# Interleaving two tensors on one core: loads and stores dealt to two DMA rings in another way

## The chip, the cores and the metric

The kernel runs on one core of one Trainium2 chip. The metric is the device time of one execution in microseconds (us). Before the change it is 314.18 us, the median of 3 runs (314.1 to 314.26).

## What is computed

```python
batch, seq, dim = 32, 256, 1024
result = np.zeros((batch, seq, dim * 2), dtype=np.float32)
result[..., 0::2] = x
result[..., 1::2] = y
```

Two fp32 tensors of 32 x 256 x 1024 (33.55 MB each) are interleaved element by element into an output of 67.11 MB. Nothing is calculated: 67.11 MB are read from HBM, put in a new order and 67.11 MB are written.

## The kernel before

**Tiles.** The work is cut into n = 8 tiles. Tile k takes 128 x 8192 elements (4.19 MB) of x and as many of y, one contiguous row of 32 KB for each of the 128 partitions, and gives 8.39 MB of output, in two halves h = 0 and 1 of 4.19 MB. SBUF holds two buffers for x (`xt[0]`, `xt[1]`), two for y (`yt`), used by tiles k in turn (k % 2), and two for the output (`ot`), one for each half: `ot[0]` takes the first half of every tile and `ot[1]` the second.

**Weaving.** VectorE (DVE) puts a half together with two copies of 128 x 4096: L67 writes x's values at the even places of `ot[h]`, L70 y's at the odd places. It goes through tiles and halves in order, so a tile has four copies. Each copy adds 1 to the semaphore `woven`, so that 4k + 2h + 2 means that half h of tile k is ready. Before L67 of tile k and half h, DVE waits for x (`xsem`, and `hsem` for the second half of x's first tile, which is loaded in two pieces), and, from tile 1 on, for `osem[h]` to reach 16k: the store of the same half of the tile before must have left `ot[h]`. Before L70 of half 0 it waits for y (`ysem`).

**Loads.** SyncE (SP) issues all of them. x's first tile goes in two halves (L42, L43), moved ahead of the opening barrier. Then come, for each tile, x (L50) and y (L53), so y0, x1, y1 right after the barrier. From tile 2 on, x waits until `woven` is 4(k-2)+3 (the last copy that reads the buffer's old x is done) and y until it is 4(k-2)+4.

**Stores.** ScalarE (ACT) issues all of them: for each half it waits until `woven` is 4k + 2h + 2 and issues the store (L83). The first half of tile 0 goes as two stores, a quarter (L77, counted by `qsem`) and three quarters (L81). Each issuing engine has a ring of its own, in which its DMAs are worked off in order: SP's is q1 in the profile and ACT's q10. So q1 carries 67.11 MB of loads and q10 67.11 MB of stores.

**The end.** ACT waits for `osem[0]` and clears the semaphores (L90); SP waits for `osem[1]`, the very last store (L91).

Of the kernel before, what the change touches and what calls it, by code (L numbers as in the profile page):

```python
# [3 lines left out]


def _interleave(nc, x, y, out):
    P = 128
    W = 8192
    H = W // 2  # L10

    total = 1
    for s in x.shape:
        total *= s
    n = total // (P * W)
    assert n * P * W == total

    def rows(ap, names, k):
        flat = ap.rearrange("b s d -> (b s d)")
        return flat[k * names : (k + 1) * names].rearrange("(p w) -> p w", p=P)  # L20

    fp32 = mybir.dt.float32
    xt = [nc.alloc_sbuf_tensor(f"xt{b}", [P, W], fp32).ap() for b in (0, 1)]
    yt = [nc.alloc_sbuf_tensor(f"yt{b}", [P, W], fp32).ap() for b in (0, 1)]
    ot = [nc.alloc_sbuf_tensor(f"ot{b}", [P, W], fp32).ap() for b in (0, 1)]

    xsem = [nc.alloc_semaphore(f"xsem{b}") for b in (0, 1)]
    hsem = nc.alloc_semaphore("hsem")
    qsem = nc.alloc_semaphore("qsem")
    ysem = [nc.alloc_semaphore(f"ysem{b}") for b in (0, 1)]  # L30
    woven = nc.alloc_semaphore("woven")
    osem = [nc.alloc_semaphore(f"osem{b}") for b in (0, 1)]


    cuts = [0, W // 4, W]
    parts = [slice(a, b) for a, b in zip(cuts, cuts[1:])]

    xs = [rows(x, P * W, k) for k in range(n)]
    ys = [rows(y, P * W, k) for k in range(n)]
    os_ = [rows(out, 2 * P * W, k) for k in range(n)]  # L40

    nc.sync.dma_start(out=xt[0][:, :H], in_=xs[0][:, :H]).then_inc(xsem[0], 16)  # L42
    nc.sync.dma_start(out=xt[0][:, H:], in_=xs[0][:, H:]).then_inc(hsem, 16)  # L43

    for k in range(n):
        b = k % 2
        if k >= 2:
            nc.sync.wait_ge(woven, 4 * (k - 2) + 3)
        if k:
            nc.sync.dma_start(out=xt[b], in_=xs[k]).then_inc(xsem[b], 16)  # L50
        if k >= 2:
            nc.sync.wait_ge(woven, 4 * (k - 2) + 4)
        nc.sync.dma_start(out=yt[b], in_=ys[k]).then_inc(ysem[b], 16)  # L53

    for k in range(n):
        b = k % 2
        for h in (0, 1):
            c = slice(h * H, (h + 1) * H)
            if h == 0:
                nc.vector.wait_ge(xsem[b], 16 * (k // 2 + 1))  # L60
            elif k == 0:
                nc.vector.wait_ge(hsem, 16)
            if k:
                nc.vector.wait_ge(osem[h], 16 * k)
            if (k, h) == (1, 0):
                nc.vector.wait_ge(qsem, 16)
            nc.vector.tensor_copy(out=ot[h][:, 0::2], in_=xt[b][:, c]).then_inc(woven, 1)  # L67
            if h == 0:
                nc.vector.wait_ge(ysem[b], 16 * (k // 2 + 1))
            nc.vector.tensor_copy(out=ot[h][:, 1::2], in_=yt[b][:, c]).then_inc(woven, 1)  # L70

    for k in range(n):
        for h in (0, 1):
            nc.scalar.wait_ge(woven, 4 * k + 2 * h + 2)
            if (k, h) == (0, 0):
                for c in parts[:-1]:
                    nc.scalar.dma_start(  # L77
                        out=os_[k][:, c], in_=ot[h][:, c]
                    ).then_inc(qsem, 16)
                c = parts[-1]  # L80
                nc.scalar.dma_start(out=os_[k][:, c], in_=ot[h][:, c]).then_inc(osem[h], 16)  # L81
                continue
            nc.scalar.dma_start(  # L83
                out=os_[k][:, h * W : (h + 1) * W], in_=ot[h]
            ).then_inc(osem[h], 16)

    nc.scalar.wait_ge(osem[0], 16 * n)
    used = sorted(s.num for s in [*xsem, hsem, qsem, *ysem, woven, osem[0]])
    assert used == list(range(used[0], used[-1] + 1)), used
    nc.scalar.sem_clear(range(used[0], used[-1] + 1))  # L90
    nc.sync.nop(nofuse=True).wait_op(osem[1], 16 * n, "sem-ge").then_inc(  # L91
        osem[1], -16 * n
    )


def kernel(tc, x, y, out):
    nc = tc.nc
    tc.close()
    tc.compile()

    _interleave(nc, x, y, out)

    blocks = nc.main_func.blocks
    for engine in (mybir.EngineType.SP, mybir.EngineType.SP):
        opening = blocks[0].instructions
        at, moved = next(
            (b, i)
            for b in blocks[1:]
            for i in b.instructions
            if i.engine == engine and i.opcode == "DMACopy"  # L110
        )
        assert not (moved.sync_info and moved.sync_info.on_wait)
        body = at.instructions
        body.remove(moved)
        gate = next(
            n
            for n, i in enumerate(opening)
            if i.engine == engine and i.opcode == "Drain"
        )
        opening.insert(gate, moved)  # L120
        at.instructions = body
        blocks[0].instructions = opening


# [1 line left out]
_INS = ['x', 'y']  # L126
_OUTS = [((32, 256, 2048), 'float32')]


# [23 lines left out]
```

## Time and profile before

| what | value |
|---|---|
| time, median of 3 runs | 314.18 us |
| span of the profiled execution | 312.9 us |
| around the span (median less span; the profiled execution has no time of its own on record) | about 1.3 us |
| bytes moved | 134.22 MB, mean 429 GB/s over the span |
| DVE | 72.0 us busy (23%), 32 copies of 2.29 us |
| DVE idle before L67, waiting for stores | 206.5 us in 14 waits |
| share of 16 engines' span: q1 (SP), q10 (ACT) | 50.1%, 49.7% |

A DMA here is 128 rows, spread over the core's 16 DMA engines, 8 rows for each engine. The profile counts a row as a packet (8, 16, 24 or 32 KB), and 16 small ones for each DMA besides: 34 DMAs x (128 + 16) = 4896 packets. "DMA share" in a stretch is the mean busy share of the 16 engines. A packet is counted where it starts, so the rate in a short stretch is rough.

### The profile page before, as it was taken

To read this page: it belongs to the slowest core of one execution; us is meant where nothing else is said; L and a number is where in the kernel's file an instruction comes from. 1 tells how busy PE (TensorE), PEld (TensorE's weight loads), DVE (VectorE), ACT (ScalarE), POOL (GpSimd) and SP (SyncE) were. 2 spreads that over 40 slices of the span, in tenths; PEclk is the share of its full clock that TensorE was granted. 3 is DMA by queue.
4 is the path that set the end of the run, shared out by engine and by line. 5 is a ranking of instruction groups with operands and counts; after the bars stand their busy time and mean duration, and the time that the engine had idled before them with its cause. 6 is when DMAs were issued, how large, how long until landed. Compare 5 with 4: busy or idle time off the path is not lost.

```text
span 312.9 us, 114 instructions
## 1 busy us (share of the span) xinstructions
DVE 72.0 (23%) x32; POOL 0.2 (0%) x4
## 2 busy tenths in 40 slices
DVE  0216000501305023050220503205032050415410
POOL 0000000000000000000000000000000000000000
DMA  8999999999999999999999999999999999999998
GB/s 337 467 402 436 436 402 419 452 457 415 427 444 411 461 402 469 402 469 402 469 402 465 406 440 432 423 448 402 469 402 469 402 469 402 469 402 448 423 423 381
DMA packets 4896, 134.22 MB, mean 429 GB/s; under 512 B 544, under 2 KB 544, under 8 KB 544
## 3 DMA queue, kind: packets, MB, share of 16 engines
q1 hardware_dynamic: 2448, 67.11, 50.1%
q10 hardware_dynamic: 2448, 67.11, 49.7%
HBM read 67.11 MB, written 67.11 MB: 429 GB/s over the span
## 4 chain that ended last, share of the span: by engine, by line
DMA 82%; DVE 12%; issue 0%
DMA out_dram<-ot 76%; DMA yt<-in_y_dram 6%; DVE ot L70 6%; DVE ot L67 6%
## 5 line engine op out<-in xcount | busy, mean ns | idle before, releaser
L67 DVE COPY ot<-xt 128x4096 f32<-128x4096 f32 x16 | 36.7, 2295 | 213.8 <-DMA out_dram<-ot 206.5
L70 DVE COPY ot<-yt 128x4096 f32<-128x4096 f32 x16 | 36.6, 2288 | 12.3 <-DMA yt<-in_y_dram 12.3
L137 POOL MEMSET const-bfloat16-1.0<- 128x1 bf16 x1 | 0.1, 103 | 0.0
L137 POOL MEMSET const-uint8-127<- 128x1 uint8 x1 | 0.1, 102 | 0.0
L137 POOL MEMSET const-float32-0.0<- 128x1 f32 x1 | 0.1, 100 | 0.2 <-issue 0.2
L137 POOL MEMSET const-float32-1.0<- 128x1 f32 x1 | 0.1, 99 | 0.0
## 6 DMA issues: line engine op xcount, KB each, us to landing
out_dram<-ot ACTq DMA_DIRECT2D x15, 4096.0 KB, 34.1
yt<-in_y_dram SPq DMA_DIRECT2D x8, 4096.0 KB, 41.5
xt<-in_x_dram SPq DMA_DIRECT2D x7, 4096.0 KB, 24.3
xt<-in_x_dram SPq DMA_DIRECT2D x2, 2048.0 KB, 9.5
out_dram<-ot ACTq DMA_DIRECT2D x1, 3072.0 KB, 32.8
out_dram<-ot ACTq DMA_DIRECT2D x1, 1024.0 KB, 16.3
```

The lines of the kernel that those rows point to most:

```text
L67: nc.vector.tensor_copy(out=ot[h][:, 0::2], in_=xt[b][:, c]).then_inc(woven, 1)
L70: nc.vector.tensor_copy(out=ot[h][:, 1::2], in_=yt[b][:, c]).then_inc(woven, 1)
L137: nc = _bacc.Bacc("TRN2", target_bir_lowering=False, num_devices=1)
```

## The change

The diff deals DMAs to the two rings by tensor and half, and no longer by direction. SP issues x's loads and the stores of half 0; ACT issues y's loads and the stores of half 1. On each engine the order is load k+1, store k, for k = 0 to 7. The waits' thresholds for loads and stores stay. The last tile isn't woven into `ot` but into `xt[0]` and `yt[0]`, the input buffers of tile 6, and so DVE waits there for its own last copy of tile 6 (`woven` at 28) and not for the stores of tile 6. The copies, the buffers, the tile size and the two small stores at the start stay.

```diff
+    nc.scalar.dma_start(out=yt[0], in_=ys[0]).then_inc(ysem[0], 16)
+
+    spare = (xt[n % 2], yt[n % 2])
+
+    def woven_to(k, h):
+        return spare[h] if k == n - 1 else ot[h]
+
+    def store(engine, k, h):
+        engine.wait_ge(woven, 4 * k + 2 * h + 2)
+        if (k, h) == (0, 0):
+            for c, sem in zip(parts, (qsem, osem[h])):
+                engine.dma_start(out=os_[k][:, c], in_=ot[h][:, c]).then_inc(sem, 16)
+            return
+        engine.dma_start(out=os_[k][:, h * W : (h + 1) * W], in_=woven_to(k, h)).then_inc(
+            osem[h], 16
+        )
+
+    def load(engine, t, sem, rows_, k, last):
+        if k >= 2:
+            engine.wait_ge(woven, 4 * (k - 2) + last)
+        engine.dma_start(out=t[k % 2], in_=rows_[k]).then_inc(sem[k % 2], 16)
 
     for k in range(n):
-        b = k % 2
-        if k >= 2:
-            nc.sync.wait_ge(woven, 4 * (k - 2) + 3)
-        if k:
-            nc.sync.dma_start(out=xt[b], in_=xs[k]).then_inc(xsem[b], 16)
-        if k >= 2:
-            nc.sync.wait_ge(woven, 4 * (k - 2) + 4)
-        nc.sync.dma_start(out=yt[b], in_=ys[k]).then_inc(ysem[b], 16)
+        if k + 1 < n:
+            load(nc.sync, xt, xsem, xs, k + 1, 3)
+            load(nc.scalar, yt, ysem, ys, k + 1, 4)
+        store(nc.sync, k, 0)
+        store(nc.scalar, k, 1)
 
     for k in range(n):
         b = k % 2
...
-            if k:
+            if k == n - 1:
+                nc.vector.wait_ge(woven, 4 * k)
+            elif k:
                 nc.vector.wait_ge(osem[h], 16 * k)
             if (k, h) == (1, 0):
                 nc.vector.wait_ge(qsem, 16)
-            nc.vector.tensor_copy(out=ot[h][:, 0::2], in_=xt[b][:, c]).then_inc(woven, 1)
+            nc.vector.tensor_copy(out=woven_to(k, h)[:, 0::2], in_=xt[b][:, c]).then_inc(woven, 1)
             if h == 0:
                 nc.vector.wait_ge(ysem[b], 16 * (k // 2 + 1))
-            nc.vector.tensor_copy(out=ot[h][:, 1::2], in_=yt[b][:, c]).then_inc(woven, 1)
-
-    for k in range(n):
-        for h in (0, 1):
-            nc.scalar.wait_ge(woven, 4 * k + 2 * h + 2)
...
-            nc.scalar.dma_start(
-                out=os_[k][:, h * W : (h + 1) * W], in_=ot[h]
-            ).then_inc(osem[h], 16)
+            nc.vector.tensor_copy(out=woven_to(k, h)[:, 1::2], in_=yt[b][:, c]).then_inc(woven, 1)
```

On the engines this means: DVE has the same 32 copies in the same order; ACT issues 16 DMAs where it had 17 (8 loads and 8 stores); SP issues 18 where it had 17 (9 loads of x, 9 stores).

More of the change, by code (lines that the diff above doesn't have):

```diff
@@ L66, in _interleave @@
                 nc.vector.wait_ge(qsem, 16)
-            nc.vector.tensor_copy(out=ot[h][:, 0::2], in_=xt[b][:, c]).then_inc(woven, 1)
+            nc.vector.tensor_copy(out=woven_to(k, h)[:, 0::2], in_=xt[b][:, c]).then_inc(woven, 1)
             if h == 0:
                 nc.vector.wait_ge(ysem[b], 16 * (k // 2 + 1))
-            nc.vector.tensor_copy(out=ot[h][:, 1::2], in_=yt[b][:, c]).then_inc(woven, 1)
-    for k in range(n):
-        for h in (0, 1):
-            nc.scalar.wait_ge(woven, 4 * k + 2 * h + 2)
[L75 to L83, printed above, removed]
-                out=os_[k][:, h * W : (h + 1) * W], in_=ot[h]
-            ).then_inc(osem[h], 16)
+            nc.vector.tensor_copy(out=woven_to(k, h)[:, 1::2], in_=yt[b][:, c]).then_inc(woven, 1)
     nc.scalar.wait_ge(osem[0], 16 * n)
```

## The prediction, as it was put on record

> **What bounds the kernel now.** I read the page's DMA rows first, then the chain, then the rate stretch by stretch, then the timeline at the two ends.
>
> ```profile
> DMA  8999999999999999999999999999999999999998
> DMA packets 4896, 134.22 MB, mean 429 GB/s; under 512 B 544, under 2 KB 544, under 8 KB 544
> q1 hardware_dynamic: 2448, 67.11, 50.1%
> q10 hardware_dynamic: 2448, 67.11, 49.7%
> DMA 82%; DVE 12%; issue 0%
> ```
>
> The 16 DMA engines are busy in every slice; the two rings together take 99.8% of the span. The chain names DVE for 12%, but only because a store follows a copy: while those copies run, the other ring and the store before keep the engines busy, as these stretches show (length, busy time of DVE and POOL, clock, DMA share, GB/s):
>
> ```profile
> 12.20:26.60 14.40, 4.69 (x3) 0.00 (x0) 1.00 1.01 437
> 26.60:32.60 6.00, 2.01 (x1) 0.00 (x0) 1.00 0.93 366
> 58.00:270.40 212.40, 49.04 (x22) 0.00 (x0) 1.00 1.01 434
> 293.50:303.20 9.70, 4.50 (x2) 0.00 (x0) 1.00 1.00 432
> ```
>
> The first has loads alone on one ring, the third loads and stores on two, the last stores alone on one. All move 432 to 437 GB/s: direction and the number of rings make no difference here. Only the second, where the stores begin, is slower. So the bound is bytes over a rate that stands still. From the chain:
>
> ```profile
> 115.53 0.02 issue
> 154.25 0.02 issue
> 192.98 0.02 issue
> ```
>
> A tile of 16.78 MB (four DMAs) takes 38.72 us, so one DMA 9.68 us and one packet of 32 KB on one engine 38.72 / 32 = 1.21 us.
>
> **Where the span's other time is.** x0 and y0 (8.39 MB) have landed at 21.89 us. Two DMAs at 9.68 are 19.36, so 2.5 us go to the start: the first issue, the ramp and the first landing. The other 30 DMAs take 312.9 - 21.9 = 291.0 us and would take 30 x 9.68 = 290.4 at the steady rate: 0.6 us are lost, and the stretch 26.6:32.6 says where. Span = 2.5 + 32 x 9.68 + 0.6 = 312.9. (34 issues, but three are pieces: 32 times 4.19 MB.)
>
> **The change, part by part.**
>
> 1. *Bytes, packets, copies.* The same DMAs of the same shapes and the same 32 copies. 0.
>
> 2. *Issues.* ACT takes eight loads, SP nine stores. An issue is 0.33 to 0.46 us (timeline rows of SP and ACT). Each lies behind a wait for `woven` and ahead of a ring that still holds other work, so 0; without such work it would cost its own 0.4 us. The stores' new waits on SP (4k+2) have x of tile k+2 queued behind them, which waits for 4k+3 anyway; on ACT the store and y behind it wait for the same 4k+4. Neither wait delays an issue by itself.
>
> 3. *The new order in each ring.* SP: x0 (two pieces), x1, s00 (two pieces), x2, s10, x3, s20, ...; ACT: y0, y1, s01, y2, s11, y3, .... It costs something only when both rings are empty at once. How the rings share is seen in the stretch 31:40, where SP's ring held loads and ACT's the quarter store:
>
> ```profile
> q1 hardware_dynamic: 107, 2.98, 77.5%
> q10 hardware_dynamic: 107, 0.79, 20.7%
> ```
>
> As many packets of each, whatever their size. So I follow the rings packet by packet, an engine having 8 of each DMA (0.61 us for 16 KB, 0.3 for 8, 0.91 for 24, 1.21 for 32). At about 3 us (SP's first issue after the barrier is at 1.90, and x0's first packets come 1 us after theirs, the rate in the first us being 16 GB/s) y0 joins x0's first piece, which has 7 packets left: 7 pairs of 1.82 us, it lands at 15.7; y0 lands at 17. x0's second piece (16 KB) pairs with y1 and lands at about 30, y1 at 31.4. The first half is woven at about 20; its store waits in the ring behind x1. The second half can be woven only at 30 to 34.7. ACT's ring is empty from 31.4 to 34.7, but SP's has x1. Then s01 and y2 pair with x1 (to 46), s00's quarter (8 pairs of 1.51, to 58) and its rest; y2 is in at about 65.6, s00 at 70.2. ACT's ring is empty again, and x2 runs alone from 70.2 to 79.9. Meanwhile tile 1 is woven: four copies, 9.0 us, 70.2 to 79.2; s10 is issued after two of them at 74.7, s11 and y3 at 79.2. So SP's ring goes over from x2 to s10 at 79.9 without a hole.
>
> From there both rings run in step: s1, then x3 and y3 (19.4 us, the cover of the 9.0 us of weaving), s2, and so on: 24 DMAs x 9.68 = 232.3 us to 312.2, plus what the stores' start loses. Cost of the order: 0.
>
> 4. *The last tile in `xt[0]`, `yt[0]`.* Now x7 and y7 land together, at about 273, and s60, s61 run until about 292 with nothing behind them if tile 7 had to wait for `ot`. That would leave both rings dry for two copies, 4.5 us. With the free buffers tile 7 is woven at 273 to 282, and s70, s71 are queued 10 us ahead. So this edit earns nothing against before, where the second-last store covers the weaving (next fence): it takes away a cost of 4.5 us which edit 3 makes.
>
> ```profile
> 283.90 2.30 DVE L67 COPY ot<-xt 128x4096 f32<-128x4096 f32 x1 [8.95 <-DMA out_dram<-ot]
> 286.11 2.29 DVE L70 COPY ot<-yt 128x4096 f32<-128x4096 f32 x1
> 293.53 2.29 DVE L67 COPY ot<-xt 128x4096 f32<-128x4096 f32 x1 [5.14 <-DMA out_dram<-ot]
> ```
>
> The store of tile 7's first half is issued at 288.4 and its forerunner lands at 293.5: there was never a hole.
>
> 5. *The stores' start, 0.6 us.* The trace can't tell whether it belongs to the first use of ACT's ring, which now falls into the ramp (then -0.6, up to -0.8 if y0 helps the ramp as well), or to the first stores (then 0, they still start), or to any ring that starts again from empty (ACT's at 34.7 and 79.2: +0.6). I take 0, the middle, and keep -0.8 and +0.6.
>
> 6. *The end.* ACT's clearing of semaphores follows s70, which lands no later than s71 since SP's ring began first; 0, or about 0.1 us if the two land together.
>
> **Sum:** 312.9 + 0 = 312.9 span, + 1.3 around it = 314.2 us, the median before.
>
> **The rivals.**
>
> *Faster: 0.13.* The start loss goes with the early first use of ACT's ring and the ramp shrinks: 314.2 - 0.8 = 313.4. For it: the loss stands where ACT's ring is first used. Against: the rate of 432 to 437 in all other stretches leaves nothing else to gain.
>
> *Slower, a hole at 80 us: 0.15.* Mechanism: s10 starts late, and x2, alone in the rings, ends before it. It decides when s10's first packet comes more than 79.9 - 74.7 = 5.2 us after its issue. The one store in the trace issued while DVE was still weaving speaks for it: L77 at 24.24, and q10 has no packet in the stretch 24.2:28.6; the copies end at 28.6.
>
> ```profile
> 24.24 0.38 ACTq L77 DMA_DIRECT2D out_dram<-ot  x1
> 24.64 0.46 ACTq L81 DMA_DIRECT2D out_dram<-ot  x1
> 26.32 2.29 DVE L70 COPY ot<-yt 128x4096 f32<-128x4096 f32 x1
> ```
>
> If 4.4 us is a delay from the issue, s10 comes at 79.1, in time by 0.8 us. If stores wait for DVE's copies, it comes at 79.2, in time by 0.7. If the 4.4 us follow the copies, it comes at 83.6: 3.7 us lost, 317.9. A smaller miss gives 315 to 316.
>
> *Slower, two loads side by side: 0.10.* Before, x and y never load at the same time. Now x and y of one tile do, row for row, in nearly all of the loading. If this is slower than 433 GB/s, some 12 DMAs (50.3 MB) pay: at 413, the rate of the stretch 27:42, 121.9 in place of 116.2 us, +5.7, so 320; at 366, the slowest row above, +21, so 335. Against it: the rate stood still whatever was mixed, and the 16 engines read 16 rows at once already.
>
> The Trainium skill, "DMA: Bandwidth & Descriptors", in "Latency and other measured facts", speaks for this rival: copies whose rows lie a large power of two apart fell to half of the rate (103 against 207 GB/s each way at 4 MiB), and x and y are each 2^25 bytes long. No run here shows it; by its halving, those 50.3 MB would cost an estimated 116 us more.
>
> **How the numbers follow.** Forecast, no change: 0.62, at 314.2. Faster 0.13, the hole 0.15, two loads 0.10. A difference of 0.2% (0.63 us) is about what a measurement of this kernel tells from none. Faster by more than that is 0.13; slower is 0.15 + 0.10 = 0.25; within is 0.62. The range goes from 313.4 (the faster case) to 316.4, which holds item 5's +0.6 and the smaller holes; it leaves out the two loads (0.10) and the large hole (about 0.05).
>
> **What would show it.** Right: DMA at 9 in every slice; s10 landing near 99 us; then a landing of stores every 38.7 us; the stores' ends at 309 to 313. The hole: a slice near 80 us with a lower digit, and later landings shifted by it. Two loads: periods of more than 38.7 us, the excess in the stretches in which both rings load. Faster: no stretch below 430 GB/s where the stores begin. The forecast is wrong if both rings are empty anywhere, or if the rate depends on what the two rings carry.

## The result, and the profile after

In twelve executions each, the kernel before takes 314.25 us in the median (314.10 to 314.46) and the changed kernel 322.41 us (314.84 to 327.01). The ratio is 1.0076, with a 95% interval of 1.0050 to 1.0103; it leaves out the six of the twelve executions that were over 1.5% longer than its shortest. What the change brings first of all is thus a spread: the same program takes 314.9 us once and 326 the next time, where the kernel before stays within 0.4 us; in 49 more executions of it, timed beside the runs below, it takes 314.10 to 314.45 us.

The profiled execution is one of the short ones: 314.94 us, span 313.6. Its page, in the lines that answer to those of before:

```profile
DMA  8999999999999999999999999999999999999997
DMA packets 4896, 134.22 MB, mean 428 GB/s; under 512 B 544, under 2 KB 544, under 8 KB 544
q1 hardware_dynamic: 2592, 67.11, 50.1%
q10 hardware_dynamic: 2304, 67.11, 49.6%
DMA 77%; DVE 11%; another core or an unknown queue 2%; issue 0%; SPq 0%; DVEq 0%
```

Full in every slice, with the two rings at 99.7% of the span. Both rings carry the same bytes; q1 has 2 x 144 more packets (both pieces of x's first tile and both of the first store). The chain, in which a tile's last store releases DVE (start, length, what):

```profile
103.97 0.03 issue
...
142.73 0.02 issue
...
181.49 0.02 issue
```

A tile takes 38.76 us here, against 38.72. A long stretch in the middle, in the windows' columns (length, DVE, POOL, clock, DMA share, GB/s), moves as much as before:

```profile
100.00:290.00 190.00, 50.84 (x23) 0.00 (x0) 1.00 1.00 433
```

The place of the hole that the prediction feared, in the timeline and in the DMA queues of the stretch 72:80 (packets, MB, share):

```profile
71.75 2.30 DVE L87 COPY ot<-xt 128x4096 f32<-128x4096 f32 x1 [41.70 <-DMA out_dram<-ot]
73.95 2.29 DVE L90 COPY ot<-yt 128x4096 f32<-128x4096 f32 x1
76.16 2.29 DVE L87 COPY ot<-xt 128x4096 f32<-128x4096 f32 x1
76.27 0.33 SPq L57 DMA_DIRECT2D out_dram<-ot  x1
```

```profile
DMA packets 104, 3.41 MB, mean 426 GB/s; under 512 B 0, under 2 KB 0, under 8 KB 0
## 3 DMA queue, kind: packets, MB, share of 16 engines
q1 hardware_dynamic: 104, 3.41, 98.6%
```

x2 is alone in the rings, as forecast (72 to 81 us, forecast 70.2 to 79.9); the store of tile 1's first half is issued at 76.27 and lands at 96.8, and there is no hole. And the last tile, woven into the free buffers while tile 6 is still being stored:

```profile
271.24 2.30 DVE L87 COPY xt<-xt 128x4096 f32<-128x4096 f32 x1 [7.64 <-DMA xt<-in_x_dram]
278.55 2.29 DVE L90 COPY xt<-yt 128x4096 f32<-128x4096 f32 x1 [5.01 <-DMA yt<-in_y_dram]
280.76 2.29 DVE L87 COPY yt<-xt 128x4096 f32<-128x4096 f32 x1
```

So from 46 us on this execution went much as the prediction worked it out (y2 lands at 69.5 us against 65.6, the rest is closer). Before that it did not: y0's first packets start at 5.7 to 6.4 us, not at 3, and the first landings are 4 to 8 us off (x0's first piece 10.9 us against 15.7 forecast, y0 20.7 against 17, x0's second piece 25.5 against 30, y1 39.5 against 31.4). No ring runs dry there, so the sum did not feel it. The execution is 0.7 us longer than before. Worked out from the packets' starts and durations, as the rates below are that stand outside the fences, 392 GB/s are moved in the stretch 35 to 45 us, where the stores begin: a loss of 0.95 us against 0.58 before. The three tiles from 104 to 220 us take 38.76, 38.76 and 38.84 us, 0.2 us more together. What makes the median 8 us longer isn't in it.

### The profile page after: what moved, and what is told of

It is laid out like the page before. It is cut to its first block, busy times and chain, and to the rows that moved or that the text cites. A ratio compares the mean times of both kernels' runs of the same rounds, so it can differ in the third digit from the quotient of the medians.

```text
span 313.6 us, 114 instructions
## 1 busy us (share of the span) xinstructions
DVE 72.0 (23%) x32; POOL 0.2 (0%) x4
## 4 chain that ended last, share of the span: by engine, by line
DMA 77%; DVE 11%; another core or an unknown queue 2%; issue 0%; SPq 0%; DVEq 0%
DMA out_dram<-ot 56%; DMA xt<-in_x_dram 15%; DMA yt<-in_y_dram 6%; DVE ot L87 4%; DVE ot L90 4%; DVE xt L87 1%; DVE xt L90 1%; DVE yt L90 1%; DVE yt L87 1%; SPq L55 0%; DVEq L86 0%
## 5 line engine op out<-in xcount | busy, mean ns | idle before, releaser
L87 DVE COPY ot<-xt 128x4096 f32<-128x4096 f32 x14 | 32.1, 2295 | 193.1 <-DMA out_dram<-ot 179.7
L90 DVE COPY ot<-yt 128x4096 f32<-128x4096 f32 x14 | 32.0, 2289 | 7.5 <-DMA yt<-in_y_dram 7.5
L87 DVE COPY xt<-xt 128x4096 f32<-128x4096 f32 x1 | 2.3, 2296 | 7.6 <-DMA xt<-in_x_dram 7.6
L90 DVE COPY xt<-yt 128x4096 f32<-128x4096 f32 x1 | 2.3, 2295 | 5.0 <-DMA yt<-in_y_dram 5.0
L87 DVE COPY yt<-xt 128x4096 f32<-128x4096 f32 x1 | 2.3, 2287 | 0.0
L90 DVE COPY yt<-yt 128x4096 f32<-128x4096 f32 x1 | 2.3, 2286 | 0.0
```

Source lines behind the costliest of these rows:

```text
L87: nc.vector.tensor_copy(out=woven_to(k, h)[:, 0::2], in_=xt[b][:, c]).then_inc(woven, 1)
L90: nc.vector.tensor_copy(out=woven_to(k, h)[:, 1::2], in_=yt[b][:, c]).then_inc(woven, 1)
```

## Experiments

Below, the *lag* is the time between the first and the last of the 16 landings of one DMA: each of the 16 DMA engines adds 1 to the DMA's semaphore when its part has landed, and the trace has the time of each.

### A longer execution: again_1 and again_2

No edit; two more executions of the changed kernel, with their profiles.

> The changed kernel once more, to see one execution's stretches. Its 12 times lie between 314.8 and 327.0 us, and the one profiled took 314.9 and kept 433 GB/s in all stretches but the start of the stores. If a stretch has both rings empty (the hole), this execution shows a low DMA share there, some us at one place, and 9.68 us for each DMA elsewhere. If loads or stores side by side are slow, the tile's period grows evenly (from 38.7 to about 40 us for a time of 325), and the excess lies in the stretches where both rings load (or both store).

> The same kernel as again_1, a second look, with the same expectations: a hole is one place with a low DMA share; a slower rate is a longer period in every tile. If it takes 315 us, it shows nothing new.

326.34 and 326.36 us. The page of again_1:

```profile
span 325.0 us, 114 instructions
...
DMA  9999999999999999999999999999999999999951
...
q1 hardware_dynamic: 2592, 67.11, 48.5%
q10 hardware_dynamic: 2304, 67.11, 48.1%
```

There is no hole: the digits are full until the 38th slice, and then fall to 5 and 1. The windows around that place:

```profile
100.00:290.00 190.00, 46.94 (x22) 0.00 (x0) 1.00 1.00 430
290.00:313.00 23.00, 5.42 (x3) 0.00 (x0) 1.00 0.96 416
313.00:324.00 11.00, 0.00 (x0) 0.00 (x0) 1.00 0.12 51
```

For 313 us, the time in which the other execution is done, this one is nearly as busy (430 against 433 GB/s in the long window). Then 11 us follow at a share of 0.12: two of 16 engines (0.125) still work, and the rest have nothing left. Here is how tiles 3 to 6 go (DVE's first copy of each):

```profile
138.53 2.29 DVE L87 COPY ot<-xt 128x4096 f32<-128x4096 f32 x1 [30.01 <-DMA out_dram<-ot]
...
180.11 2.29 DVE L87 COPY ot<-xt 128x4096 f32<-128x4096 f32 x1 [31.10 <-DMA out_dram<-ot]
...
221.92 2.30 DVE L87 COPY ot<-xt 128x4096 f32<-128x4096 f32 x1 [30.86 <-DMA out_dram<-ot]
...
263.34 2.29 DVE L87 COPY ot<-xt 128x4096 f32<-128x4096 f32 x1 [31.43 <-DMA out_dram<-ot]
```

41.4 to 41.8 us for a tile and not 38.7: DVE waits for the slowest engine's part of each store. The landings show the rest: in both executions the lag on SP's ring is 0.7 to 0.9 us at 81 us, 2.0 at 98, and grows with every DMA to 13 at 284 us, with one or two engines behind and fourteen within 0.5 us of each other. The records don't name the engines, but the packets of again_1 can be strung together into 16 chains that leave no gaps; fourteen end at 312.6 to 313.1 us and two at 323.8 and 324.6. From 60 us on 64 packets of 32 KB took more than 1.23 us, up to 2.42; in the short execution 13 did, up to 1.35, and in the kernel before one, 1.25. What the 64 took beyond 1.21 us adds up to 24 us, about what the two late engines lose together (11 and 12): longer packets are their delay, and no waiting.

What follows: neither of the two expectations. There is no hole and no stretch that is slow for all engines; some packets are held up, most of all on one or two engines, and these fall behind.

### Is it loads, or stores, side by side? loads_two and stores_two

loads_two has three buffers each for x and y, leaves out the weaving, and stores one tile alone:

```diff
+    for k in range(2 * n):
+        load(nc.sync, xt, xsem, xs, k, k % n)
+        load(nc.scalar, yt, ysem, ys, k, (k + 0) % n)
```

stores_two loads one tile, leaves out the weaving, and then stores:

```diff
+    for k in range(n):
+        nc.sync.dma_start(out=os_[k][:, :W], in_=xt[0]).then_inc(osem[0], 16)
+        nc.scalar.dma_start(out=os_[k][:, W:], in_=yt[0]).then_inc(osem[1], 16)
```

> Loads alone: each of x and y is loaded twice over, x by SP's ring and y by ACT's side by side, three buffers each, so that each ring always has work; no weaving, and only two stores of 4.19 MB at the end (the output is left unwritten but for one tile). 32 loads and 2 stores at 9.68 us are 329 us, and about 332 to 333 with the start and the last landings. By the theory that two loads side by side are slow, it takes over 340 us, or its times spread by some per cent from one execution to the next as the changed kernel's do; by the others (a hole, two stores side by side) it takes 332 with a spread under 0.3%.

> Stores alone: one tile of x and of y is loaded, and then all 16 halves of the output are stored from these two buffers, half 0 by SP's ring and half 1 by ACT's, side by side (nothing is woven, the output is not interleaved). 2 loads and 16 stores at 9.68 us are 174 us, about 177 with start and end. By the theory that two stores side by side are slow, it takes over 180 us or its times spread by some per cent; by the others 177 with a spread under 0.3%.

336.7 to 337.0 us and 181.7 to 181.9 us: 4 and 5 us over the figure, and neither spreads. stores_two is also over the 180 us that were to speak for slow stores, so its rate has to decide. The middle stretch of loads_two, and then that of stores_two:

```profile
23.30:314.70 291.40, 0.00 (x0) 1.00 1.00 430
```

```profile
42.90:179.00 136.10, 0.00 (x0) 1.00 1.00 431
```

A pair of loads lands every 19.43 us and a pair of stores every 19.44: 9.72 us for a DMA, 0.4% more than the 9.68 of mixed work, and no engine falls behind (the lag is 0.6 us at 62 us and at 315). A part of the rest is the wait between the loads and the first store that needs them, which the figures left out (1.2 to 1.8 us in stores_two, in which the engines stand still); another is the start, as the first pair lands at 23 us. What follows: the rival of slow loads side by side is out, and that of slow stores. The power-of-two rule of the Trainium skill ("DMA: Bandwidth & Descriptors", "Latency and other measured facts"), weighed in the prediction, does not show here: x and y side by side load at 430 GB/s. How far apart the two lie in memory no trace shows.

### One ring loading while the other stores: out_of_phase

New theory (switch): engines are held up where all of them go over from loading to storing, or back, on both rings at about the same time.

```diff
-    cuts = [0, W // 4, W]
+    cuts = [0, W]
...
+        elif t is yt:
+            engine.wait_ge(xsem[1], 16)
         engine.dma_start(out=t[k % 2], in_=rows_[k]).then_inc(sem[k % 2], 16)
...
```

> The changed kernel with the first store whole and with y's second tile held back until x's second has landed, so that from about 29 us on one ring loads while the other stores. The order of DMAs in each ring stays. Theory (switch): two of the 16 DMA engines fall behind by about 1.5 us in each tile where all engines go over from storing to loading on both rings at once; with one ring loading and one storing at all times, as before the change, nobody falls behind: 313.5 to 315 us, a spread under 0.3%, and the 16 landings of each DMA within 0.6 us to the end. Rival (a ring that carries both directions in turn disturbs): times still spread from 315 to 327.

314.64 to 314.94 us in eight of ten executions, and 315.42 and 316.52; ratio to before 1.0023 (1.0012 to 1.0035).

```profile
DMA  9999999999999999999999999999999999999998
```

```profile
50.00:290.00 240.00, 60.91 (x28) 0.00 (x0) 1.00 1.01 434
```

The lag is 0.6 us at 56 us and at 313. Two of the ten are over the 315 us that were expected. But for the first store, which is whole here, the rings carry the same DMAs in the same order as in the changed kernel. What follows: that a ring carries both directions in turn is not enough to make the spread. Two things were changed, though, the phase and the first store, and the kernel with the whole store alone (whole_store, below) is as steady in eight of ten; this run doesn't tell the two apart, and the runs with two engines set back have to. Nor is the phase wholly opposite. SP's ring turns at 87.1, 106.5 and 125.8 us and ACT's at 94.4, 113.7 and 133.1, so the rings go in opposite directions for 12 of each 19.4 us and in the same one for 7. In the changed kernel ACT's ring also turns 7 us after SP's (104.0 after 96.8, 123.4 after 116.1), but the same way: both load or both store for 12 us, and for 7 they are mixed. The 0.5 us that it is behind the kernel before stand where the stores begin (387 GB/s from 25 to 35 us, 1.07 us lost against 0.58).

### Turning on one ring: one_ring

```diff
-    nc.scalar.dma_start(out=yt[0], in_=ys[0]).then_inc(ysem[0], 16)
+    nc.sync.dma_start(out=yt[0], in_=ys[0]).then_inc(ysem[0], 16)
...
-            load(nc.scalar, yt, ysem, ys, k + 1, 4)
+            load(nc.sync, yt, ysem, ys, k + 1, 4)
         store(nc.sync, k, 0)
-        store(nc.scalar, k, 1)
+        store(nc.sync, k, 1)
...
```

> The changed kernel's order of DMAs, all on SP's ring: loads of x and y, then both stores, in turn; ACT issues none. Every engine still goes over from loading to storing and back every 19.4 us. By the switch theory two engines fall behind here as well, and the times lie above 317 or spread by over 1%. By the rival that it takes two rings side by side, nobody falls behind: pure stretches cost 9.72 a DMA (loads_two, stores_two), so 32 x 9.72 + 3 = 314 to 315.5, spread under 0.3%.

315.55 to 318.17 us, six executions, median 317.14. In the profiled one (317.35) the lag grows from 0.7 us at 110 us to 3.0 at 287, with two to four engines behind. This fits neither expectation well: a lag, but a quarter of that of again_1, and three of six times above 317. It shows where packets are held up: 52 of its 54 that took more than 1.23 us after 60 us start within 2 us of the landing of the first part of a load of y (80.5, 119.2, 158.0, 196.8, 235.5, 274.3 us), where the ring goes from loads to stores.

### The first store in one piece: whole_store

```diff
-    cuts = [0, W // 4, W]
+    cuts = [0, W]
...
```

> The changed kernel with the first store in one piece of 4.19 MB and not in 1.05 and 3.15. The pieces put SP's ring 7 us ahead of ACT's in the changed kernel, so that 7 of each 19.4 us are mixed; whole, the rings should go over more nearly together. Switch theory: engines still fall behind, times from 315 to 330 with a spread over 1%. Rival (the stragglers come from the 8 KB packets of the small store): 314 to 315 with a spread under 0.3%.

314.70 to 315.06 us in eight of ten executions, and 316.53 and 317.93; ratio 1.0034 (1.0013 to 1.0055). The one profiled is the longest, and its lag grows from 0.5 us at 83 to 6.1 at 299. So the stragglers are there without the 8 KB packets, but much rarer and slower to grow, and the expectation missed on that. With the whole store no ring runs alone around 75 us, and ACT's ring is about 5 us ahead of SP's and not 7 behind.

### Without the free buffers: no_spare

```diff
-        return spare[h] if k == n - 1 else ot[h]
+        return ot[h]
...
-            if k == n - 1:
-                nc.vector.wait_ge(woven, 4 * k)
-            elif k:
+            if k:
```

> The changed kernel with the last tile woven into ot, as before, so that its copies wait for tile 6's stores. In the trace of the changed kernel SP's ring is 7 us ahead of ACT's at the end (stores of tile 6 land at 290.6 and 297.9), so that SP's ring is empty while ACT's still has work; ACT's is empty while SP's store of tile 7 runs. By the prediction's item 4 a hole of up to 4.5 us; with the 7 us between the rings, each covers the other, so 0 to 2 us. The spread of the changed kernel stays (315 to 328).

317.24, 317.47, 319.06, 329.16 and 330.25 us. The shortest is 2.4 us over the changed kernel's shortest. The profile is of the longest, in which one engine lags by 13 us:

```profile
285.00:305.00 20.00, 1.45 (x1) 0.00 (x0) 1.00 0.41 175
```

Before the last tile the other fifteen engines run out of work and wait until the straggler has landed its part of tile 6's store. So the free buffers are worth 2.4 us to this order, if the two shortest executions can be compared, and in a long one 328.9 - 325.0 = 3.9 us of span. The prediction had 4.5. All five executions are on one chip, and they spread like the changed kernel's.

### Setting two engines back: seed_after, seed_out_of_phase, seed_before, seed_loads

If being out of step is what costs, then an engine that is put out of step must pay in every execution. Two rows of a DMA fall on two engines:

```diff
+    R = 2
...
+    spill = nc.alloc_sbuf_tensor("spill", [P, 4000], fp32).ap()
...
+        if k == 1:
+            for r in range(R):
+                nc.sync.dma_start(out=spill[2 * r : 2 * r + 2], in_=xs[0][2 * r : 2 * r + 2, :4000]).then_inc(ssem, 16)
...
```

> The changed kernel with two small extra loads behind the store of tile 1's first half, each of two rows of 16,000 bytes into a scratch tile that nothing reads; with two rows they should fall on two of the 16 engines only and set these back by 2 x 0.6 = 1.2 us at about 100 us. Switch theory: an engine that is out of step with the others is held up each time the others turn, so the two fall further behind in every execution: lag growing from 1.2 us to 8 us and more, all times above 319. Rival (chance stalls that have nothing to do with being out of step): 1.2 us more than the changed kernel, spread between 316 and 328 as before, and the lag stays at 1.2 us where the execution is a short one.

> The same two extra loads in out_of_phase, where one ring loads while the other stores. Switch theory: the lag of 1.2 us stays as it is to the end, 315.9 to 316.2 us in nearly all runs. If any lagging engine is slowed whatever the others do, it grows to several us, 319 and more.

> The same two extra loads in the kernel before, on SP's ring behind y's fourth tile. Switch theory: loads and stores are mixed on all engines at all times, the lag of 1.2 us stays to the end: 315.4 to 315.6 us, spread under 0.3%. If any lagging engine is slowed whatever the others do: 319 and more.

> The same two extra loads in loads_two, behind its sixth pair of loads: a pure stream of loads on two rings, in which nothing turns until the end. Switch theory: the lag of 1.2 us stays, 338.1 us. If a lagging engine is slowed in a pure stream as well, the landings of one DMA drift apart from 1.8 us to several us by 310 us.

| kernel | without the two loads, us | with them, us |
|---|---|---|
| changed kernel | 314.84 to 327.01 | 325.82 to 327.74 |
| out_of_phase | 314.64 to 316.52 | 316.27 to 316.55 |
| before | 314.10 to 314.46 | 317.77 to 319.89 |
| loads_two | 336.73 to 337.03 | 338.87 to 338.92 |

The page and the end of seed_after:

```profile
DMA  9999999999999999999999999999999999999951
...
q1 hardware_dynamic: 2600, 67.17, 48.6%
q10 hardware_dynamic: 2304, 67.11, 48.0%
```

```profile
313.00:324.00 11.00, 0.00 (x0) 0.00 (x0) 1.00 0.12 51
```

These are the rows of again_1 once more, and now all four executions are as long as it. The lag of the DMA on SP's ring that lands nearest to each time, in us:

| kernel | at 80 us | 120 | 165 | 205 | 245 | 285 |
|---|---|---|---|---|---|---|
| before | 0.2 | 0.3 | 0.2 | 0.2 | 0.2 | 0.2 |
| after, the short execution | 0.4 | 0.4 | 0.5 | 0.6 | 0.6 | 0.6 |
| again_1 | 0.7 | 2.6 | 4.9 | 7.9 | 10.3 | 13.2 |
| seed_after | 0.5 | 6.8 | 9.0 | 11.7 | 14.0 | 14.0 |
| seed_out_of_phase | 1.8 | 6.8 | 6.7 | 6.6 | 6.6 | 6.5 |
| seed_loads | 0.5 | 0.5 | 6.2 | 6.2 | 6.2 | 6.2 |
| seed_before | 0.4 | 0.4 | 6.9 | 7.6 | 8.0 | 8.6 |

The first jump is larger than 1.2 us because the extra packets take their turns against ACT's, the small one that ends each DMA too: the two rows on an engine start 3 to 4 us apart, time for a row and two packets of 1.21. So the two engines fall about 6 us behind on SP's ring and get 1 to 3 us ahead on ACT's. What they cost by themselves is read from seed_loads and seed_out_of_phase, 2.0 and 1.6 us, and not 1.2. What counts is what happens after: in a pure stream of loads the lag stands still for 150 us, and with the rings in opposite phase as well; in the changed kernel it goes on growing, on ACT's ring too (1.6 us at 163, 10.1 at 286), and costs 11.5 us over a short execution. In the kernel before it grows a little, and costs 3.5 to 5.6 us, more than the 1.2 that was expected: an engine out of step isn't free there either, though no ring turns, and two of the four times are over the 319 that were to mean that a lagging engine is slowed whatever the others do. Turning rings are thus not all that holds it up. But nothing in that kernel puts an engine out of step.

### What it takes: seed_one_ring, seed_half_tiles, seed_whole_store

The first is one_ring and the third whole_store, each with the two extra loads; the second is seed_after with

```diff
-    W = 8192
+    W = 4096
...
-        if k == 1:
+        if k == 3:
```

> one_ring with the two small extra loads of seed_after behind the stores of tile 1. Switch theory (turning in unison is enough, one ring or two): the two engines set back by 1.2 us fall further behind at the turns, 8 us and more, all times above 319. Rival (it takes two rings side by side): the lag stays, 2 us more than one_ring's 315.6 to 318.2.

> seed_after with tiles of half the size (W = 4096, 16 tiles, DMAs of 2.10 MB), the two extra loads behind the store of tile 3's first half, at about the same time. The engines turn every 9.7 us and not every 19.4. If the lag grows by an amount for each turn (about 1.2 us in seed_after), the two engines lose twice as much, some 24 to 30 us, and since the others can run ahead by no more than about one tile, the time is 335 to 345. If it grows with time or bytes, whatever the number of turns, it is 326 to 328 again.

> whole_store (eight of its ten times within 314.7 to 315.1) with the two small extra loads of seed_after. If its steady time is only for want of an engine out of step, the two extra loads bring all runs to 319 and more, the lag growing at each turn as in seed_after. If the whole first store does away with the cause itself, the lag stays and the time is 316.5 to 317.5, as in out_of_phase.

seed_one_ring: 318.27 to 318.58 us. The lag is 3.5 us from 123 to 229 us and 4.2 from 240 to the end. So the switch theory in its first form falls: turning together on one ring holds up an engine that is far behind once or twice, not at each turn. Small lags come on one ring as well (one_ring); the large ones take two.

seed_half_tiles: 331.04, 332.62, 335.65 and 335.77 us. Two are in the 335 to 345 of a loss for each turn and two below it; all are clear of the 326 to 328 of a loss with time. Its middle stretch:

```profile
100.00:290.00 190.00, 42.55 (x36) 0.00 (x0) 1.00 1.00 412
```

All engines are busy at a share of 1.00, and yet they move 412 GB/s in place of 430 to 433: packets take longer. At 206 us four engines lag, by 8 to 11 us. The lag doesn't double (12.1 us at most, against 16.4 in seed_after), and it isn't the extra loads' doing alone: it is 3.0 us at 61 us and 4.6 at 82, and their first packets come at 88. Half tiles without the extra loads were not run, so what the smaller DMAs cost by themselves is open. It fits a loss for each turn, but doesn't show it.

seed_whole_store: 317.32, 317.60, 320.71 and 320.72 us. Two executions cost 2.5 us and two 5.8 over whole_store's usual 314.9. This doesn't decide: the 7.1 us that the extra loads make shrink to 2.3 at 160 us, and a lag then grows (5.1 at 180, 8.9 at 300), more slowly than in the changed kernel. So whole_store lacks the first lag, and pays less for one, though its rings turn 5 us apart and not 7: turning more nearly together isn't what makes it worse.

## Why the prediction was wrong

**The bound and the sum** held for the execution that it describes. Steps 1, 2 and 6 stand: no DMA, copy or issue costs anything by itself, and the short execution ends at 313.6 us against 312.9 forecast. Step 4 is right in kind, but the free buffers save 2.4 to 3.9 us and not 4.5, as x7 and y7 don't land together (271.2 and 278.5 us). Only four of the twelve executions lie in the forecast's range, and that the one profiled was among them was luck. Where the engines stay in step, the rate doesn't depend on what the rings carry by more than 0.4% (9.72 against 9.68 us a DMA).

**Step 3 failed.** It followed the rings "packet by packet, an engine having 8 of each DMA", and took what one engine does for what all sixteen do: "From there both rings run in step", "Cost of the order: 0". Nothing in the program keeps the 16 engines in step; each works off its own part of both rings. In the kernel before they stay within 0.3 us of each other from 47 us on. In again_1 and again_2 one or two fall behind, by about 1.2 us in each half period of 20 us (0.7 to 13.2 us between 81 and 284 us), and the kernel ends with the slowest of them, 12 us later. That the other long ones (six of the twelve over 325 us, and two at 319) are of this kind is inferred from their times.

What was shown: set back by the two extra loads, two engines fall far behind, and all four executions are long (seed_after); with the rings mostly in opposite directions (seed_out_of_phase) or without turns (seed_loads) the lag stays where it is; with one ring the large loss goes (seed_one_ring). The traces also show when packets are held up. In the short execution the 13 long packets start at 79.3, 115.4 to 115.8, 154.2 to 154.5 and 193.0 to 193.3 us, where the first parts of x's loads land (80.6, 115.7, 154.4, 193.2), and the stores behind them begin; the twelve after the first are loads of y, which ACT's ring still carries there. In whole_store, where ACT's ring turns first, 29 of its 30 start within 3.5 us of that ring's turn to stores, and all 30 are on SP's ring. In out_of_phase one packet took over 1.23 us (1.24). In the long executions the late engines are also held up after the turn back to loads (97.8 and 136.0 to 138.1 us in again_1, after 96.3 and 135.1).

So the cost belongs to two rings that load together, turn to stores one soon after the other and turn back, and to an engine that is out of step with the others there. What sets the first engine back was not shown.

**Step 5** asked where the 0.6 us of the stores' start belong. To the first stores: ACT's ring carries y0 from 5.7 us on and 5 to 35 us run at 432 to 434 GB/s, and the loss comes when the first stores begin. It is 0.95 us and not 0.58 in the short execution.

**The rivals.** The hole did not come, though x2 was alone just as worked out: 433 GB/s from 75 to 85 us. Two loads side by side cost 0.4%, not 5%. The faster case was out, since the start's loss grew. The case that came, a spread that begins in single engines, was none of them. The trace of before could not show it directly, as its rings never turn; but the prediction should have priced the loss of a state that it relied on without naming it, sixteen engines in step.

**What stays open.** Why a packet is held up when the others turn: the trace has its duration, not its cause. How the loss depends on the distance between the two rings' turns. Why only some of the executions get a first lag: in again_1, again_2 and no_spare it appears at 79 to 81 us, where x2 has run alone and SP's ring turns to stores on all engines, and whole_store, which has no such place, is steady in eight of ten; that is an argument and was not tried by itself. The traces have one sign earlier: at 58 us two engines, one and one are 1.6 to 2.0 us late on SP's ring in these three, as many as lag afterwards, and one is 1.5 us late in the short execution; at 71 us this is gone in all four (0.4 to 0.5 us). Which engines they are the records don't say. The Trainium skill ("DMA: Bandwidth & Descriptors", "Latency and other measured facts") notes two of the 16 as usually slower, and by its best guess at the cause this is specific to DMAs issued from GpSimd, of which this kernel has none. Here one or two lag unprompted, while two set back by the extra loads lag just as well.

No version tried beats the kernel before: the best, out_of_phase, is at 1.0023 (1.0012 to 1.0035).

## What to carry to other kernels

When a transfer-bound kernel is full at every slice, the order of its DMAs is still not free: ask whether the DMA engines stay in step, and read the spread of one DMA's 16 landings over the run, not only the last of them. Loads on one ring and stores on the other keep each engine on an even mix nearly all the time. Dealing both directions to both rings lets all engines turn together; here it helped to hold the rings in opposite phase for most of the time. And time a changed kernel in a dozen executions before its profile is read: here the one profile showed nothing of an 8 us longer median.

## What the runs showed of the hardware that was not expected

- The 16 engines can drift apart under two rings that turn together: packets of 1.21 us took up to 2.42 us, two engines of again_1 ended 11 us late, and the fourteen others ended when all do in a short execution.
- Packets are held up where loads give way to stores: in the short execution, one_ring and whole_store nearly all that took more than 1.23 us after 60 us lie at such a turn.
- A mixed stream (9.68 us for 4.19 MB) is 0.4% faster than pure loads or pure stores on two rings (9.72).
- Where the first stores join running loads, 0.6 to 1.1 us of transfer are lost: 0.58 us before, 0.95 after, 1.07 in out_of_phase. In stores_two, where no load runs at that point, the first stores' packets are only some 0.3 us longer on each engine.
- A DMA of two rows falls on two engines: the two extra ones set back two engines and left the other fourteen as they were.
